# Two transformer blocks on one core: the scheduler's timing model exchanged, the program text unchanged

## The chip, the cores and the metric

The kernel runs on one core of a Trainium2 chip. The metric is the device time of one execution in microseconds; a comparison goes by the median of several runs. TensorE is called PE below, its weight loads PEld, VectorE DVE, ScalarE ACT, GpSimd POOL, SyncE SP.

## What is computed

One sequence of 512 tokens with 1024 features goes through two blocks of two layers each, all in float32. Cut to what matters:

```
first_block, per layer:                     # "block 1"
  u = rmsnorm(h) @ w_in                     # q, kv, rope, gates, GLA inputs
  y = [ MLA attention(u) * silu(gate_a),
        gated linear attention(u), two directions, chunks of 64, * silu(gate_g) ]
  h += y @ w_out
  h += sigmoid(rmsnorm(h) @ w_ple_gate) * (p @ w_ple_proj)
h = rmsnorm(h, final_norm)
second_block, per layer:                    # "block 2"
  u = rms_norm(h) @ w_in
  attn = dilated attention(rope(q), rope(k), v), three patterns, 8 heads
  dn   = gated delta rule(silu(conv(q, k, v))), 4 heads, chunks of 64:
         T = (I + A)^-1 by triangular solve, then a scan over 8 chunks
  h += rms_norm([attn, rms_norm(dn) * silu(z)] @ w_out)
  h += rms_norm((gelu(conv(gate)) * conv(up)) @ ffn_w_out)   # FFN of 2816
```

## The kernel before

Tokens lie in four tiles of 128 (`NT`); features are cut into eight blocks of 128 (`KT`). A float32 product is made from three matmuls of reduced type, in `mm3` (L178 to L181): high part by high part (L179), and the two mixed products (L180, L181). Operands are therefore split into a high part, cast on ACT (`split`, L263, and for weights L143), and a rest, subtracted on DVE (L264, L144).

Every weight comes through `take` (L130 to L146): SP issues a load of 512 KB into `wr` (L140, two buffers), ACT casts it to `wh` (L143), DVE subtracts to get `wl` (L144), four buffers each.

The places that the prediction speaks of, in the order of the program:

- `norm_t` (L329 to L340) normalizes one token tile in two halves: two squares with sums on ACT (L296), POOL forms the root (L297, L299), DVE writes `xn` (L335, two buffers, so that one tile at a time is held), and PE transposes it in eight pieces through `flip` (L274). The next tile's L296 writes its junk into the same `xn`.
- `gla_gate` (L495 to L509) of block 1: PE forms `ps_z` (L497), ACT takes absolute value, exponential and logarithm (L499 to L501) and the rest (L503), DVE adds and scans (L504 to L508).
- The delta rule of block 2. DVE solves 16 by 16 pieces in 30 dependent operations (L1043, L1045); ACT issues eight stores of them to the DRAM tensor `dT` (L1047). `q_rows` (L1051 to L1064) has short matmuls on `th`, a square that ACT makes (L1053 to L1056), and L1060, whose product DVE takes in L1061. `merges` (from L1104) loads T for one head back through ACT's queue (L1109), transposes it on PE (`ps_d`, L274), copies it on ACT (L1114), and builds the full inverse by L1120 to L1129. Then come the eight scan steps (L1145 to L1168): L1151 needs the state `S`; DVE adds (L1152); L1160 forms `ps_dS` from that; DVE adds it to the state (L1161), for the next L1151. L1154 and L1167 also use it, beside this chain.
- The set-up of the dilated attention (L1190 to L1195): ACT casts the keys (L1190), SP moves the halves across partitions (L1191), DVE subtracts (L1192), SP moves that (L1193). Scores are formed in L1220 and L1221.
- `add_norm` and `norm_t` for each token tile before the FFN, and the FFN itself.

What sets the order: each engine runs its own queue strictly in the order in which the instructions stand there, and waits at semaphores. That order isn't written by hand. The text gives each instruction a priority, its place in the program, which `tc.high_priority(offset=...)` moves forward; the scheduler steps through a timing model of the engines and lets each engine take, of what its model holds ready, what has the best priority. A few lines steer it:

```
with tc.high_priority(offset=lead[0]):        # every weight, in take()
...
with tc.high_priority(offset=600):
    oN = merges()
```

`lead[0]` is set stage by stage (30, 5, 80, ...), so weights come that much ahead of the work around them. The change touches `kernel`, L1446.

## Time and profile before

| | |
|---|---|
| median of 3 runs | 2128.76 us (2126.56 to 2129.99) |
| the profiled execution | 2130.51 us |
| its span, first to last instruction | 2128.4 us |
| mean granted TensorE clock | 0.996 |
| PE, PEld, DVE busy | 2037.4, 1685.4, 1279.2 us |
| ACT, POOL busy | 959.2, 194.9 us |
| DMA | 209.41 MB, 98 GB/s on the mean |

The sum in the prediction is made against the profiled execution, 1.75 us above the median. A matmul's duration in a row overlaps the next one's, since they are pipelined; the distance between two starts tells what one costs the queue.

### The profile page before, as it was taken

What the parts mean: (1) busy time and instruction counts of PE and PEld (TensorE: products, weight loads), DVE (VectorE), ACT (ScalarE), POOL (GpSimd) and SP (SyncE); (2) the same over time, 40 slices, a digit from 0 to 9 for tenths busy, and PEclk for the clock granted to TensorE, in tenths of its full rate; (3) what the DMA queues carried; (4) which work ended last, traced back from release to release, by engine and by line L of the source; (5) the groups of instructions that cost most, each with busy time, mean ns of one, the idle gap of its engine ahead of it and who ended that gap; (6) DMA issues with size and microseconds to landing.
All of it is one profiled execution on the core that took longest, in us unless ns stands there. A gap on an engine that the chain in (4) does not pass through costs nothing.

```text
span 2128.4 us, 28253 instructions
## 1 busy us (share of the span) xinstructions
PE 2037.4 (96%) x10792; PEld 1685.4 (79%) x10792; DVE 1279.2 (60%) x2218; ACT 959.2 (45%) x1805; POOL 194.9 (9%) x337
## 2 busy tenths in 40 slices
PE   7899999999999899999999999999999999999998
PEld 6687878778877888777788888878887678888886
DVE  6667655667844676575666425567757646662364
ACT  4745444635634553255544324346333654442342
POOL 1110001111000111200200000021112020000001
PEclk9999999999999999999999999999999999999999
DMA  5232233322133531141633333243211244332332
GB/s 170 85 92 70 70 109 118 104 80 87 44 127 103 173 95 58 45 114 51 188 109 99 92 96 99 70 152 113 79 55 50 75 146 142 99 97 92 99 99 89
DMA packets 74038, 209.41 MB, mean 98 GB/s; under 512 B 16624, under 2 KB 17648, under 8 KB 73392
## 3 DMA queue, kind: packets, MB, share of 16 engines
q1 hardware_dynamic: 62896, 202.89, 31.1%
q10 hardware_dynamic: 11008, 4.72, 0.9%
q8 instruction: 85, 1.39, 0.3%
q14 instruction: 49, 0.40, 0.1%
HBM read 182.16 MB, written 17.04 MB: 94 GB/s over the span
## 4 chain that ended last, share of the span: by engine, by line
PE 75%; DVE 7%; ACT 6%; DMA 5%; issue 3%; POOL 3%; POOLq 0%; SPq 0%; ACTq 0%; DVEq 0%
PE ps_mm L180 19%; PE ps_mm L181 18%; PE ps_mm L179 18%; DMA wr<-in_w 4%; DVE wl L144 2%; PE ps_tr L274 2%; ACT wh L143 2%; PE ps_o L1243 1%; ACT xn L296 1%; PE ps_mo L179 1%; PE ps_mo L180 1%; PE ps_pt L274 1%; PE ps_mo L181 1%; POOL r2h L297 1%; PE ps_pv L1151 1%
## 5 line engine op out<-in xcount | busy, mean ns | idle before, releaser
L144 DVE TENSOR_TENSOR wl<-wr,wh 128x1024 fp32r<-128x1024 f32 (+4 forms) x304 | 360.7, 1189 | 395.4 <-ACT wh L143 389.7
L143 ACT CAST wh<-wr 128x1024 fp32r<-128x1024 f32 (+4 forms) x304 | 309.3, 1019 | 357.1 <-PE ps_mm L181 151.3
L180 PE MATMUL ps_mm<-wl,xh 128*128 128x512 f32 (+2 forms) x736 | 282.6, 385 | 9.3 <-DVE wl L144 9.2
L181 PE MATMUL ps_mm<-x2h,wl 128*128 128x512 f32 (+1 forms) x768 | 285.5, 372 | 0.0
L180 PE MATMUL ps_mm<-x2l,wh 128*128 128x512 f32 (+1 forms) x768 | 285.4, 372 | 0.0
L179 PE MATMUL ps_mm<-x2h,wh 128*128 128x512 f32 (+1 forms) x768 | 285.4, 372 | 0.0
L179 PE MATMUL ps_mm<-wh,xh 128*128 128x512 f32 (+2 forms) x736 | 282.7, 386 | 2.1 <-ACT wh L143 1.7
L181 PE MATMUL ps_mm<-wh,xl 128*128 128x512 f32 (+2 forms) x736 | 280.9, 382 | 0.0
L180 PEld LDWEIGHTS ps_mm<-wl,xh 128*128 128x128 f32 x736 | 139.9, 190 | 37.5 <-DVE wl L144 15.0
L181 PEld LDWEIGHTS ps_mm<-x2h,wl 128*128 128x128 f32 x768 | 144.7, 188 | 25.1
L180 PEld LDWEIGHTS ps_mm<-x2l,wh 128*128 128x128 f32 x768 | 144.7, 188 | 25.0
L179 PEld LDWEIGHTS ps_mm<-x2h,wh 128*128 128x128 f32 x768 | 144.7, 188 | 24.9
L179 PEld LDWEIGHTS ps_mm<-wh,xh 128*128 128x128 f32 x736 | 139.5, 190 | 28.8 <-ACT wh L143 4.8
L181 PEld LDWEIGHTS ps_mm<-wh,xl 128*128 128x128 f32 x736 | 139.7, 190 | 23.3 <-issue 0.7
L1336 DVE SCALAR_TENSOR_TENSOR rt<-ps_mm,par,rt 128x511 f32<-128x511 f32 (+1 forms) x176 | 131.3, 746 | 3.0
L179 PE MATMUL ps_mm<-xh,wh 128*128 128x512 f32 x320 | 127.0, 397 | 0.9 <-DVE rp L358 0.9
L180 PE MATMUL ps_mm<-xl,wh 128*128 128x512 f32 x320 | 126.4, 395 | 0.0
L181 PE MATMUL ps_mm<-xh,wl 128*128 128x512 f32 x320 | 126.4, 395 | 0.0
L297 POOL TENSOR_SCALAR r2h<-ss 128x1 f32<-128x1 f32 x48 | 18.9, 393 | 995.0 <-ACT th L296 759.6
L180 PE MATMUL ps_mm<-wl,hh 128*128 128x512 f32 x224 | 89.1, 399 | 0.6 <-DVE wl L144 0.5
L179 PE MATMUL ps_mm<-wh,hh 128*128 128x512 f32 x224 | 88.2, 395 | 0.3 <-ACT wh L143 0.3
L181 PE MATMUL ps_mm<-wh,hl 128*128 128x512 f32 x224 | 88.0, 394 | 0.0
(401 smaller groups left out, 3798.3 us busy)
## 6 DMA issues: line engine op xcount, KB each, us to landing
wr<-in_w SPq DMA_DIRECT2D x270, 512.0 KB, 3.6
gain<-in_gain SPq DMA_DIRECT2D x13, 512.0 KB, 6.3
wr<-in_w SPq DMA_DIRECT2D x14, 384.0 KB, 3.1
x<-in_x SPq DMA_DIRECT2D x8, 512.0 KB, 5.9
wm<-gqk SPq DMA_DIRECT2D x32, 128.0 KB, 2.3
xd<-x SPq DMA_DIRECT2D x8, 512.0 KB, 2.6
xs<-xd SPq DMA_DIRECT2D x8, 512.0 KB, 3.9
xs<-xm SPq DMA_DIRECT2D x8, 512.0 KB, 4.6
```

The costliest lines, as they stand in the source:

```text
L143: nc.scalar.copy(hi[:, :n], raw[:, :n])
L144: nc.vector.tensor_tensor(lo[:, :n], raw[:, :n], hi[:, :n].bitcast(F32), ALU.subtract)
L179: nc.tensor.matmul(ps, l[0], r[0], start=start, stop=False)
L180: nc.tensor.matmul(ps, l[0], r[1], start=False, stop=False)
L181: nc.tensor.matmul(ps, l[1], r[0], start=False, stop=stop)
L274: nc.tensor.transpose(ps[:w, tsl(j)], src[:, tsl(j, w)], ident)
L296: nc.scalar.activation(junk[i], halves[i], AF.Square, accum_out=ss[:, i:i + 1])
L297: nc.gpsimd.tensor_scalar(r[:, i:i + 1], ss[:, i:i + 1], 1.0 / D, r[:, 0:1] if i else EPS, ALU.mult, ALU.add)
L1151: nc.tensor.matmul(pv[rs, tsl(h)], wT[h][:, cs], S[:, h], start=True, stop=True)
L1243: nc.tensor.matmul(o[tsl(h % 2, 64), tsl(h // 2)], av[:, j, tsl(h, 64)], p_[:, tsl(i * c + j)], start=j == 0, stop=j == qt)
L1336: nc.vector.scalar_tensor_tensor(acc[:, j:], ps[:, :SEQ - j], par[:, w0 + 3 * m + 2 - j:w0 + 3 * m + 3 - j], acc[:, j:], ALU.mult, ALU.add)
```

## The change

One argument of the context that schedules the program. The scheduler's model of time is another; the program text, its priorities, buffers and pools stay.

```diff
--- before.py
+++ after.py
@@ -1443,7 +1443,7 @@
     args["w"] = nc.dram_tensor("in_w", (W_TOTAL,), F32, kind="ExternalInput").ap()
     out = nc.dram_tensor("out_0", (P, NT, D), F32, kind="ExternalOutput").ap()
     plan = []
-    with tile.TileContext(nc) as tc, ExitStack() as ctx:
+    with tile.TileContext(nc, schedule_with_timeline_sim=True) as tc, ExitStack() as ctx:
         body(ctx, tc, args, out, plan)
     arrays["in_w"] = weight_stream(plan, I)
     r = _run(nc, [arrays], core_ids=[0])
```

Both programs have the same instructions, in the same numbers on every engine. The queues differ: of PE's, which has 8602 rows before when neighbours of one kind are put together and 8457 now, most stretches are in another order. The separate wait instructions also differ in number: 297 before and 259 now on PE, 503 and 539 on ACT, 462 and 496 on DVE, 371 and 359 on SP, 152 and 130 on POOL.

The first place is the scan of block 2's layer 0 on PE. Names with `ps_` are accumulators in PSUM: `ps_pv`, `ps_qv`, `ps_dS` and `ps_po` are the scan's, `ps_mm` belongs to the large products. Before:

```order
L181 MATMUL ps_mm<-wh,xl 128x512
L179 MATMUL ps_mm<-wh,xh 128x512
L1160 MATMUL ps_dS<-vn,kN 128x128 x4
L1167 MATMUL ps_po<-vn,ET 128x128 x4
L180 MATMUL ps_mm<-wl,xh 128x512
L1151 MATMUL ps_pv<-S,A 64x128 x4
L1154 MATMUL ps_qv<-S,qT 64x128 x4
L1160 MATMUL ps_dS<-vn,kN 128x128 x4
L274 MATMUL ps_tr<-ident,cv 128x128 x4
L181 MATMUL ps_mm<-wh,xl 128x512
L179 MATMUL ps_mm<-wh,xh 128x512
L1151 MATMUL ps_pv<-S,A 64x128 x4
```

and now:

```order
L1151 MATMUL ps_pv<-S,A 64x128 x4
L1160 MATMUL ps_dS<-vn,kN 128x128 x4
L1151 MATMUL ps_pv<-S,A 64x128 x4
L1154 MATMUL ps_qv<-S,qT 64x128 x4
L1160 MATMUL ps_dS<-vn,kN 128x128 x4
L1167 MATMUL ps_po<-vn,ET 128x128 x4
L1151 MATMUL ps_pv<-S,A 64x128 x4
L1154 MATMUL ps_qv<-S,qT 64x128 x4
L1160 MATMUL ps_dS<-vn,kN 128x128 x4
L1151 MATMUL ps_pv<-S,A 64x128 x4
L1154 MATMUL ps_qv<-S,qT 64x128 x4
L1160 MATMUL ps_dS<-vn,kN 128x128 x4
```

The products `ps_mm` that stood between the scan's own steps are gone from it; the scan's steps follow each other.

The second place is the first use of the inverse T on PE (`ps_d` from `dt`), with the products around it. Before:

```order
L181 MATMUL ps_mm<-wh,xl 128x512
L179 MATMUL ps_mm<-wh,xh 128x512
L274 MATMUL ps_tr<-ident,cv 128x128 x4
L180 MATMUL ps_mm<-wl,xh 128x512
L181 MATMUL ps_mm<-wh,xl 128x512
L180 MATMUL ps_mm<-wl,xh 128x512
L181 MATMUL ps_mm<-wh,xl 128x512
L274 MATMUL ps_d<-ident,dt 128x128 x4
L179 MATMUL ps_mm<-wh,xh 128x512
L180 MATMUL ps_mm<-wl,xh 128x512
```

and now:

```order
L179 MATMUL ps_mm<-xh,wh 128x512
L180 MATMUL ps_mm<-xl,wh 128x512
L181 MATMUL ps_mm<-xh,wl 128x512
L1056 MATMUL ps_tr<-ones,th 128x1 x4
L1060 MATMUL ps_tr<-qT,kT 128x128 x4
L1056 MATMUL ps_tr<-ones,th 128x1 x4
L274 MATMUL ps_d<-ident,dt 128x128 x4
L1060 MATMUL ps_tr<-qT,kT 128x128 x4
L1120 MATMUL ps_d<-dt 128x128 x4
L1056 MATMUL ps_tr<-ones,th 128x1 x4
L179 MATMUL ps_mm<-wh,xh 128x512
```

The transposes of T have moved into the middle of `q_rows` (L1056, L1060), ahead of the projection products that stood before them.

The third place is ACT's queue around the stores of T (L1047) and its load (L1109). Before:

```order
L143 CAST wh<-wr 128x1024
L969 ACTIVATE th<-cv 128x512
L964 ACTIVATE cv<-ps_mm,half_w 128x512
L1047 DMA dT_6505<-dt 16x16x16 x8
L143 CAST wh<-wr 128x1024
L969 ACTIVATE th<-cv 128x512
L1109 DMA dt<-dT_6505 128x512
L964 ACTIVATE cv<-ps_mm,half_w 128x512
L1114 COPY dt<-ps_d 128x512
```

and now:

```order
L1053 ACTIVATE th<-qT 128x512
L143 CAST wh<-wr 128x1024
L1047 DMA dT_6505<-dt 16x16x16 x8
L969 ACTIVATE th<-cv 128x512
L143 CAST wh<-wr 128x1024
L1109 DMA dt<-dT_6505 128x512
L1053 ACTIVATE th<-qT 128x512
L969 ACTIVATE th<-cv 128x512
L1053 ACTIVATE th<-qT 128x512
L969 ACTIVATE th<-cv 128x512
L964 ACTIVATE cv<-ps_mm,half_w 128x512
L1114 COPY dt<-ps_d 128x512
```

Two squares of `q_rows` (L1053) now stand behind the load of T, and one ahead of the stores.

## Rows read from the trace of the kernel before

**Rows 1.** The profile page, part 1: busy time, share of the span, instructions.

```profile
PE 2037.4 (96%) x10792; PEld 1685.4 (79%) x10792; DVE 1279.2 (60%) x2218; ACT 959.2 (45%) x1805; POOL 194.9 (9%) x337
```

**Rows 2.** Windows: stretch, its length, busy us and (count) by engine, PEclk, DMA share, GB/s.

```profile
13.00:712.00 699.00, 662.35 (x3575) 550.47 (x3576) 446.77 (x818) 347.05 (x707) 73.01 (x159) 0.99 0.31 97
712.00:1055.00 343.00, 327.33 (x1964) 270.29 (x1963) 223.62 (x472) 163.28 (x356) 48.11 (x63) 1.00 0.33 96
1200.00:1300.00 100.00, 100.00 (x438) 81.76 (x437) 31.35 (x32) 28.57 (x34) 0.00 (x0) 1.00 0.33 95
1395.00:1760.00 365.00, 346.61 (x2069) 284.49 (x2069) 243.82 (x500) 178.61 (x393) 60.36 (x85) 1.00 0.32 95
```

**Rows 3.** Waits of PE: what it waited for, us in total, times, longest us.

```profile
PE ps_tr L274 <- DVE xn L335: 32.7, 22, 7.4
PE ps_mm L180 <- DVE wl L144: 10.8, 17, 2.3
PE ps_mm L179 <- ACT wh L143: 3.9, 8, 0.9
PE ps_z L497 <- ACT wa L503: 3.6, 2, 2.4
PE ps_d L1129 <- DVE dt L1126: 3.6, 2, 1.8
PE ps_pv L1151 <- DVE S L1161: 2.7, 4, 0.8
...
PE ps_mm L179 <- DVE sga L364: 2.4, 2, 1.2
...
PE ps_d L274 <- DMA dt<-dT: 1.2, 2, 0.9
```

**Rows 4.** Timeline at 405 us, PE: start, us, line, operation, [idle before, releaser].

```profile
405.78 0.79 PE L180 MATMUL ps_mm<-wl,xh 128*128 128x512 f32 x1 [2.27 <-DVE wl L144]
...
406.37 0.63 PE L181 MATMUL ps_mm<-wh,xl 128*128 128x512 f32 x1
```

**Rows 5.** Windows: after that stall, and one stretch of the scan.

```profile
405.00:410.00 5.00, 4.22 (x12) 3.37 (x13) 4.85 (x6) 4.95 (x9) 3.32 (x4) 0.66 0.61 163
890.00:906.00 16.00, 15.30 (x104) 12.60 (x104) 9.91 (x17) 0.63 (x1) 5.32 (x6) 1.00 0.00 1
```

**Rows 6.** Timeline, solver end and T load, layer 0 (ACTq and SPq: DMA issues).

```profile
813.05 5.07 ACTq L1047 DMA_DIRECT2D dT<-dt  x8
...
820.43 0.36 ACTq L1109 DMA_DIRECT2D dt<-dT  x1
...
825.54 0.59 ACT L1114 COPY dt<-ps_d 128x512 f32<-128x512 f32 x1 [4.01 <-PE ps_d L274]
```

**Rows 7.** Timeline, scan of layer 0.

```profile
890.04 1.09 PE L1151 MATMUL ps_pv<-S,A 128*64 128x128 f32 x8 [0.75 <-DVE S L1161]
...
893.28 1.16 PE L1160 MATMUL ps_dS<-vn,kN 64*128 64x128 f32 x8
...
894.37 1.16 PE L1167 MATMUL ps_po<-vn,ET 128*128 128x128 f32 x8
894.54 0.69 DVE L1161 TENSOR_TENSOR S<-S,ps_dS 128x512 f32<-128x512 f32 x1 [1.23 <-PE ps_dS L1160]
```

**Rows 8.** Timeline, set-up before the attention of layer 0.

```profile
932.08 0.60 ACT L1087 ACTIVATE akT<-ps_tr 128x512 f32<-128x512 f32 x1 [3.38 <-PE ps_tr L274]
...
936.96 0.46 SPq L1193 DMA_DIRECT2D vs<-vs  x1
```

**Rows 9.** DMA of 934 to 948 us: issue, KB each, us to landing.

```profile
vs<-vs SPq DMA_DIRECT2D x1, 512.0 KB, 4.5
...
lo<-lo SPq DMA_DIRECT2D x1, 512.0 KB, 7.3
```

**Rows 10.** Timeline, two token tiles of the norm before the FFN.

```profile
1027.85 1.32 PE L274 MATMUL ps_tr<-ident,xn 128*128 128x128 f32 x8 [1.76 <-DVE xn L335]
...
1033.80 0.66 PE L274 MATMUL ps_tr<-ident,xn 128*128 128x128 f32 x4 [0.53 <-DVE xn L335]
```

## The prediction

> **What bounds the kernel now.** I read the busy times first: PE is busy 2037.4 us of the span of 2128.4 [rows 1], DVE 1279.2, ACT 959.2. So PE's queue sets the time, and a new order can only change how long PE stands idle and at which clock it runs. The windows tell where it stands: length less busy time is 36.7 us from 13 to 712 us (block 1), 15.7 from 712 to 1055 and 18.4 from 1395 to 1760 (the mixers of block 2 with the steps around them) [rows 2]. In the stretch of the FFN, 1200 to 1300, there is none: 438 matmuls in 100 us, so one costs 0.228 us. These 70.8 us are what a better order could win at most, apart from the clock. The list of PE's waits names them: 32.7 us for normalized rows, 10.8 and 3.9 us for the two halves of a weight, 3.6 us for the gate of block 1, 3.6 us in the merges, 2.7 us in the scan, and many groups like the 2.4 us for `sga` [rows 3].
>
> To these comes the clock. After 2.27 us idle at 405.78 us the next starts are 0.59 us apart and those after them 0.43, against 0.228 [rows 2, 4]: the level of 1.2 GHz. The 5 us from 405 on have a mean clock of 0.66 [rows 5], so 5 x 0.34 = 1.7 us of work is lost. The trace has four such places (near 68, 406, 436 and 713 us), each behind a stall of over 2 us.
>
> **The change part by part.** The instructions stay; only queues move. For each wait of PE I took from the two orders its cover: the matmul work that stands in PE's queue between the last matmul that the awaited value depends on and the matmul that waits, each at its undisturbed distance. A cover longer than the chain through ACT, DVE, POOL or DMA means no stall. The sum is made against the profiled execution, 2130.5 us; it lies 1.75 us above the median of the runs.
>
> *Gains.* The new order sets work that hangs on a chain later behind more products.
> - Weights, 14.7 us in 25 waits [rows 3]: of some 145 first waits on a new weight 26 had under 4 us of cover, now 8 of 141. I take 10 us; at least 5, at most 14.7.
> - The gate of block 1, 3.6 us [rows 3]: 3 of 6 covers were under 4 us, now none. 3.6 us.
> - L1129 in the merges, 3.6 us [rows 3]: 6 of 8 covers were under 1 us, now 1 of 7. 2.6 us.
> - Groups like `sga`, 2.4 us [rows 3], all in block 1 or at the start of the mixer: covers under 4 us were in the majority and are nearly gone. Together 12 us; bounds 6 and 14.
> - Normalized rows in block 1, part of the 32.7 us [rows 3]: 11 us of it is the start, when nothing else can run, and stays; at the later places covers grow by 2 to 5 us. 4 us; bounds 0 and 10.
> - Three of the four falls of the clock follow stalls that go: 3 x 1.7 = 5.1 us.
>
> Together -37.3 us.
>
> *Losses*, all in block 2, per layer twice.
> - The trip of T. The solver's last operations on DVE now stand behind an L1061, and that needs an L1060 which ends 7.7 us of matmuls before T's transposes. From there: about 1.9 us of DVE, then 7.4 us from the first store to the load (813.05 to 820.43), then 4.4 us until its data are in (the copy behind the transposes, which take 0.66, starts at 825.54) [rows 6]. That is 13.7 against 7.7: 6 us a layer, part of it already at the L1056 ahead, whose square stands behind that load on ACT. Before, both layers paid 1.2 us [rows 3]. Net +10.8; bounds 0 (everything earlier on DVE) and 14 (with a fall of the clock in each).
> - The scan. A step's L1160 starts at 893.28, L1161 at 894.54 and lasts 0.69, so the state is there 1.95 us on, while the queue can start the next matmul 1.09 us after L1160 (894.37) [rows 7]. With nothing between, 0.9 us is lost in each of the four steps without L1167 behind them, 3.6 us a layer. Before, products stood between, and L1151 still waited 0.75 us at 890.04 [rows 7]; 2.7 us in both layers [rows 3]. Net +4.5; bounds 0 and 10.
> - The set-up of the attention. From the copy of the last key tile (932.08) to the issue of the second move (936.96) it is 4.9 us, to its landing 4.5 more [rows 8, 9]: 9.4 us. The cover falls from 14.8 us to about 6.8: 2.6 us lost. The other half's rest lands only 7.3 us after its issue [rows 9]; what that costs, behind the first stall, lies between 0 and 5, and I take the middle, 2.5. Net +10; bounds 0 and 18.
> - The norm before the FFN. The transposes of the second tile now follow those of the first with nothing between; in the trace they start 5.95 us after them (1027.85 to 1033.80) [rows 10], of which eight transposes take 0.9. PE would wait 4.5 to 5 us and lose clock; but the four tiles stall for 5.0 us already before, and the third and fourth are better covered now. Net +2; bounds -4 and +8.
> - Covers that become very short elsewhere: 59 waits have under 0.5 us, 23 before. 24 of the 36 new ones are priced above; the others, at 0.4 us (the mean of those 23 without the start), and the operands of L179 and L181 in the first output product of each layer, come to +8; bounds 0 and 15.
>
> Together +35.3 us. I cost at nothing the FFN stretches, where PE is full and DVE and ACT have room [rows 2]; without that cover their weight waits would cost as in the list, some 5 us. The fewer wait instructions on PE (38) are worth at most 2 us, left out.
>
> By places the sum is -37.3 + 35.3 = **-2 us**. I do not trust this alone: it counts gains from stalls that were measured, and losses only where a chain is visibly longer than its cover. In the trace before, such chains explain about 60 of the 110 us that starts lie apart beyond their undisturbed distance at waits; the rest fell on waits with 2 to 10 us of cover. So I made a second sum, by classes: the mean stall of a wait before was 0.58 us below 0.5 us of cover, 0.11 at 0.5 to 2, 0.14 at 2 to 5, 0.12 at 5 to 10. Their counts go from 23, 190, 384 and 207 to 59, 153, 318 and 389. That gives 139 us now: **+29 us**. This sum does not know which chains are long. I take the middle, +13.5: 2130.5 + 13.5 - 1.75 = **2142 us** as a median.
>
> A rule on the clock speaks against the change. First the row: the scan's stretch from 890 to 906 us holds 0.7 us of idle time in pieces, and its clock is 1.00 [rows 5]. The Trainium skill, "TensorE: Matmul & The Clock Gate", section "A second HAM failure mode: psum-queue depth-cycling", says that short idle spells between groups of matmuls can make the clock swing between its levels. By the row the unfilled scan costs no clock; by the rule it is the fourth rival.
>
> **The rivals.**
> 1. *The trips in block 2 stay hidden*: faster. Both large losses rest on data that go through DRAM or across partitions and on when they are issued. If ACT and DVE reach the stores of T and L1190 earlier against PE, because PE itself was held up before, the stalls vanish. It decides at a trip of 7.7 us for T and 6.8 for the keys. For it: DVE is idle 40% and ACT 55% [rows 1]. Against it: 7.4 us of T's trip are issue and stores alone [rows 6]. 2142 - 10.8 - 10 = 2121 us.
> 2. *The sum by places is right*: 2130.5 - 2 - 1.75 = 2127 us. For it: every large wait of before was followed. Against it: the 50 us that no chain foretold.
> 3. *The classes are right, or more*: 2130.5 + 29 - 1.75 = 2158 us, up to 2172 where short covers cost more than their mean. For it: the shortest class grows from 23 to 59.
> 4. *The clock falls in the scan*: about 13 us of it a layer have nothing between the steps; at half the clock they take twice as long, 2 x 13 = 26 us: 2168 us. Against it stands the clock of 1.00 [rows 5].
> 5. *The orders amount to the same*: 2129 us. The two queues hardly share a stretch, so this would be chance.
>
> **How the numbers follow.** A measurement of this kernel can tell some 0.2%, 4.3 us, from no change. Chances: the forecast (2127 to 2158 as its own range) 0.36, of which 0.05 faster, 0.05 the same, 0.26 slower; rival 1 0.21 (0.20 faster, 0.01 same); rival 2 0.15 (0.08 faster, 0.07 same); rival 3 0.21, slower; rival 4 0.05, slower; rival 5 0.02, same. Faster 0.33, same 0.15, slower 0.52. The range takes in rival 1 down to 2112 (with the norms at their better bound) and rivals 3 and 4 to 2170.
>
> **What would show it.** Right: in the windows, less idle time of PE in block 1 (some 15 us in place of 36.7) and more in each mixer of block 2; in the waits, the groups for weights, `ps_z` and `sga` nearly gone; `ps_d` L274 or the L1056 ahead of it with about 6 us a layer, L1151 with four waits of 0.9 us a layer, L1220 or L1221 with 2 to 5 us; eight transposes behind eight with a stall of over 4 us. Clock 1.00 in the scan would reject rival 4. The forecast is wrong if block 2's mixers are idle no longer than before, or if block 1's stalls return under other names for the same sum.

## The result: slower, and the profile after

| | before | the change |
|---|---|---|
| median | 2129.38 us (2126.56 to 2131.05) | 2155.19 us (2148.09 to 2158.85) |
| ratio to before, 95% interval | | 1.0119 [1.0090, 1.0147] |
| profiled execution | 2130.51 us | 2148.09 us |
| its span, mean granted clock | 2128.4 us, 0.996 | 2146.3 us, 0.981 |

The change is slower by 25.8 us. The forecast was 2142 us (2112 to 2170), 13 us above before: the sign came true and the time lies inside the range, but the loss is twice the one that was forecast. The profiled execution is the fastest of four, so its trace can explain 17.6 us; the other 8 differ from run to run, in part with the clock, as shown below.

The profile page of the change, busy times (as [rows 1]):

```profile
PE 2046.5 (95%) x10792; PEld 1718.9 (80%) x10792; DVE 1287.1 (60%) x2218; ACT 949.2 (44%) x1805; POOL 191.5 (9%) x337
```

Windows of the change over the same four stretches of work (as [rows 2]; columns: stretch, its length, busy us and count of PE, PEld, DVE, ACT, POOL, clock, DMA share, GB/s):

```profile
13.00:709.00 696.00, 668.18 (x3572) 558.78 (x3572) 450.48 (x823) 342.64 (x708) 73.42 (x159) 0.99 0.31 98
709.00:1062.00 353.00, 328.85 (x1970) 281.46 (x1969) 225.15 (x466) 160.68 (x355) 45.50 (x63) 0.97 0.32 94
1200.00:1300.00 100.00, 100.00 (x439) 81.92 (x438) 31.50 (x32) 29.03 (x35) 0.00 (x0) 1.00 0.32 95
1402.00:1777.00 375.00, 346.13 (x2047) 294.84 (x2047) 248.60 (x502) 175.15 (x390) 58.06 (x84) 0.96 0.31 95
```

Length less busy time of PE: block 1 now stands idle 27.8 us in place of 36.7, the two mixers with their steps 24.2 and 28.9 in place of 15.7 and 18.4. The FFN is full as before. The two mixer stretches also lost clock: 0.97 and 0.96 in place of 1.00.

Waits of PE in the change (as [rows 3]: us in total, times, longest):

```profile
PE ps_tr L274 <- DVE xn L335: 19.5, 5, 7.8
PE ps_pv L1151 <- DVE S L1161: 7.0, 9, 0.9
PE ps_first L181 <- DVE xl L264: 6.0, 7, 2.2
PE ps_tr L1056 <- ACT th L1053: 5.4, 2, 2.7
PE ps_dS L1160 <- DVE vn L1152: 5.4, 7, 0.9
...
PE ps_mm L179 <- ACT x2h L263: 3.8, 2, 1.9
...
PE ps_s L1221 <- DMA lo<-lo: 1.2, 2, 0.7
...
PE ps_d L1129 <- DVE dt L1126: 0.8, 1, 0.8
...
PE ps_s L1221 <- DMA vs<-vs: 0.6, 1, 0.6
```

Six of these nine groups had no row among the waits of before: `xl` for `ps_first` (the first products of a layer), the square L1053, `x2h`, both moves of the keys, and L1160.

**Where the time went.** Both programs run the same matmuls, so there are points in PE's queue at which both have run exactly the same set. Distances between these points, from the starts of matmuls in the two profiled executions, in us:

| stretch | before | change | difference |
|---|---|---|---|
| block 1 and the step into block 2, up to its first products | 764.6 | 756.6 | -8.0 |
| mixer of layer 0 (projections, T, scan) | 168.9 | 177.1 | +8.2 |
| attention of layer 0 | 65.5 | 67.3 | +1.8 |
| norm before the FFN, layer 0 | 33.3 | 37.5 | +4.2 |
| FFN of layer 0 | 359.1 | 357.8 | -1.3 |
| step to layer 1 | 22.8 | 26.6 | +3.8 |
| first products of layer 1 | 62.4 | 58.8 | -3.6 |
| mixer of layer 1 | 169.6 | 175.3 | +5.7 |
| attention of layer 1 | 66.2 | 68.7 | +2.5 |
| norm before the FFN, layer 1 | 33.0 | 37.5 | +4.5 |
| FFN of layer 1 | 358.9 | 357.4 | -1.5 |

They sum to +16.3 of the 17.9 us by which the two spans differ; the rest lies ahead of the first point and behind the last. The stretches that lost have +30.7, the forecast's losses were +35.3; those that won have -14.4, the forecast's gains were -37.3. Each of these stretches is a net of what it won and lost.

### The profile page after: what moved, and what is told of

Same layout as the page of the kernel before. It is cut to its first block, busy times and chain, and to the rows that moved or that the text cites. A ratio compares the mean times of both kernels' runs of the same rounds, so it can differ in the third digit from the quotient of the medians.

```text
span 2146.3 us, 28251 instructions
## 1 busy us (share of the span) xinstructions
PE 2046.5 (95%) x10792; PEld 1718.9 (80%) x10792; DVE 1287.1 (60%) x2218; ACT 949.2 (44%) x1805; POOL 191.5 (9%) x337
## 4 chain that ended last, share of the span: by engine, by line
PE 84%; DVE 7%; ACT 4%; DMA 2%; issue 2%; POOL 2%; SPq 0%; DVEq 0%; POOLq 0%; ACTq 0%
PE ps_mm L180 21%; PE ps_mm L179 21%; PE ps_mm L181 21%; PE ps_tr L274 2%; PE ps_o L1243 1%; DVE wl L144 1%; DMA wr<-in_w 1%; PE ps_mo L181 1%; PE ps_pt L274 1%; PE ps_mo L179 1%; PE ps_first L181 1%; PE ps_mo L180 1%; PE ps_d L1120 1%; PE ps_d L1125 1%; POOL r2h L297 1%
## 5 line engine op out<-in xcount | busy, mean ns | idle before, releaser
L179 PE MATMUL ps_mm<-x2h,wh 128*128 128x512 f32 (+1 forms) x768 | 285.6, 375 | 3.8 <-ACT x2h L263 3.8
L179 PE MATMUL ps_mm<-wh,xh 128*128 128x512 f32 (+2 forms) x736 | 274.2, 381 | 2.8 <-ACT wh L143 2.0
L179 PEld LDWEIGHTS ps_mm<-x2h,wh 128*128 128x128 f32 x768 | 145.7, 191 | 29.8 <-ACT x2h L263 4.7
L180 PEld LDWEIGHTS ps_mm<-wl,xh 128*128 128x128 f32 x736 | 139.2, 189 | 28.9 <-DVE wl L144 5.4
L179 PEld LDWEIGHTS ps_mm<-wh,xh 128*128 128x128 f32 x736 | 138.7, 189 | 27.6 <-ACT wh L143 2.7
L179 PE MATMUL ps_mm<-xh,wh 128*128 128x512 f32 x320 | 126.6, 396 | 0.1
L179 PE MATMUL ps_mm<-wh,hh 128*128 128x512 f32 x224 | 87.0, 394 | 0.0
```

Of the source, the lines that this page charges most:

```text
L179: nc.tensor.matmul(ps, l[0], r[0], start=start, stop=False)
L180: nc.tensor.matmul(ps, l[0], r[1], start=False, stop=False)
```

## Experiments

Twelve runs, in three groups, each beside fresh runs of the kernel before on its chip (medians 2131.98, 2132.31 and 2132.26 us).

**The method.** A helper chains all instructions of each engine in a given order, by edges that only order the issue. So either program's order can be held, and also a mixture: each engine follows one order up to one of the points above and the other from there on.

```diff
-    with tile.TileContext(nc, schedule_with_timeline_sim=True) as tc, ExitStack() as ctx:
-        body(ctx, tc, args, out, plan)
+    with tile.TileContext(nc) as tc, ExitStack() as ctx:
+        body(ctx, tc, args, out, plan); hold(tc)
...
+def hold(tc):
...
+        row = [own[j] for j in np.cumsum(steps)]
...
+        for a, b in zip(row, row[1:]):
+            tc.add_manual_dep(b, a.name, info, reason="order")
```

What each mixture holds; all that isn't named is in the other order:

```
first_block_new    block 1 and its step to block 2: the change's order
second_block_new   all behind that:                 the change's order
mixers_new         both mixers with attentions:     the change's order
norms_new          both norms and the start of the
                   FFN behind, step to layer 1:     the change's order
mixers_old         both mixers with attentions:     the order of before
norms_old          both norms and the start of the
                   FFN behind, step to layer 1:     the order of before
best_mix           the change's order where its stretch was the shorter: most
                   of block 1 and the first products of layer 1
```

A second tool is *pads*: n extra matmuls of the identity with itself, ahead of a matmul that waits, into the bank that it is about to overwrite. Their products are never read. They are meant to keep PE busy through a wait, and so the clock up. The code is one line of the kernel, broken up here:

```diff
+        ps = psum.tile([P, 512], F32, tag=f"b{b[i]}", name=f"ps_{role}")
+        n, at = PADAT.get(CALLS[0], (0, 0))
...
+        PADS.extend((nc.tensor.matmul(ps[:, :P], ident, ident, start=True, stop=True).ins, at) for _ in range(n))
```

### Is it the clock? Pads in the change, in before, and in block 2 alone

`new_padded`: 188 pads at 55 waits of the change. 

> The order of the change, unchanged on every engine, with 188 extra small matmuls (identity by identity, 0.27 us each, results overwritten) put in PE's queue directly ahead of 55 matmuls that stand idle by 0.5 us or more in the profile of the change. They fill idle time and remove no wait. Theory A (the clock): the 26 us of the change are time at 1.2 GHz; with PE occupied in its stalls the clock stays up, so 2128 to 2138 us, mean clock 0.99 or more. Theory B (the waits): the new order's waits themselves are the loss and the clock only shows them; then 2150 to 2160 us, since every wait is still there.

`old_padded`: 144 pads at 46 waits of before, the control. 

> The same with the order of before: 144 small matmuls ahead of 46 stalls. Control for the price of the extra matmuls themselves. Theory A: before loses about 6 us to four falls of the clock, most of them behind stalls that can be filled, so 2123 to 2128 us. Theory B: 2129 to 2135 us, nothing to gain and some matmuls that come a little late.

`new_padded_2`: 142 pads at 26 waits, only in block 2. 

> The order of the change again, with extra small matmuls only in block 2 and only ahead of 26 matmuls that stood idle by 0.85 us or more (142 of them, counted at 0.25 us against the measured idle time, so that they end about with the wait): the norms before the FFN, the L1056 behind T, the scan, three products of the attention. new_padded raised the clock to 0.988 and won nothing, but its matmuls took 63.6 us where 45.4 us of idle time went, so 18 us were its own price. Theory A (the clock costs what it shows): about 12 us of the time at the low level in block 2 goes, 2139 to 2147 us. Theory B (the stalls are set by chains on ACT and DVE, and the clock falls inside them cost little): 2151 to 2160 us.

| | median us | ratio to before [95%] | clock of the profiled run |
|---|---|---|---|
| new_padded | 2153.72 (2151.19 to 2155.93) | 1.0101 [1.0087, 1.0115] | 0.988 |
| old_padded | 2131.84 (2128.06 to 2134.85) | 0.9998 [0.9989, 1.0008] | 0.995 |
| new_padded_2 | 2149.60 (2147.68 to 2150.96) | 1.0074 [1.0061, 1.0087] | 0.991 |

Pads change nothing in before, whose clock was 0.995 already. In the change they raise the clock. `new_padded` still came out at theory B's time: its pads took more than they gave. `new_padded_2`, whose pads are fitted more closely, lies between the two theories: it wins 8 to 10 us by the ratios, 1.0074 against 1.0119 and, in a later group, 1.0112, with intervals that don't meet. Even these pads aren't free: PE's idle time (the span less its busy time) falls from 99.8 us in the change to 78.1, by 21.7 us, but the pads themselves keep PE busy for 37.8. So the clock costs the change some 8 us or more; how much more can't be read from these runs.

Not all of the low clock costs something. The norm before the FFN of layer 1, in the windows of the change:

```profile
1764.00:1775.00 11.00, 5.89 (x25) 5.20 (x26) 9.67 (x15) 6.76 (x16) 4.92 (x12) 0.53 0.83 249
```

and of `new_padded_2`, the same work:

```profile
1767.00:1778.00 11.00, 8.61 (x69) 7.78 (x69) 9.42 (x13) 6.66 (x16) 4.68 (x12) 1.00 0.82 245
```

The clock rises from 0.53 to 1.00 and the stretch stays: 37.5 us in the change, 37.8 padded (layer 0: 37.5 and 39.0). In `new_padded` the same stretch took 37.5 us in both layers, at a clock of 1.00. The timeline of `new_padded_2` shows why:

```profile
1764.82 4.41 PE L120 MATMUL ps_tr<-ident 128*128 128x128 f32 x38
...
1769.94 1.32 PE L274 MATMUL ps_tr<-ident,xn 128*128 128x128 f32 x8 [0.72 <-DVE xn L335]
1771.10 1.95 PE L120 MATMUL ps_mm<-ident 128*128 128x128 f32 x16
...
1774.08 0.74 PE L179 MATMUL ps_mm<-x2h,wh 128*128 128x256 f32 x4 [1.03 <-ACT x2h L263]
```

A pad leaves two rows, as any float32 product does. With 19 pads (x38) through the wait for `xn` and 8 (x16) behind the transposes PE still waits 0.72 and 1.03 us at the ends: the chain through DVE and ACT sets this place, at either clock. The Trainium skill, "TensorE: Matmul & The Clock Gate", section "HAM oscillation — how this bites in real kernels", prices time at the lower clock at half its length; for these 11 us at 0.53 that would be some 5 us, an estimate. The trace doesn't agree: the measured price here is nothing.

### Which part? Blocks held apart

`first_block_new` 

> Block 1 up to the first products of block 2 in the order of the change on all engines, everything behind it in the order of before. By the two profiles the change is 8 us ahead at that point, with about as many falls of the clock as before: 2118 to 2125 us (theory A and B alike). The prediction's terms for block 1 alone would give some 2104 us.

`second_block_new` 

> The mirror: block 1 in the order of before, block 2 in that of the change. If the two halves add up, 2155 + 8 = 2163 us, 2156 to 2167. Theory A: mean clock at or below 0.985, with falls at the same places of block 2 as in the change. Theory B: clock near 0.99 and PE idle by 25 us more than before.

Measured: 2126.30 us (2123.50 to 2128.58), 0.9972 [0.9960, 0.9983], and 2161.73 us (2158.14 to 2164.44), 1.0138 [1.0124, 1.0152]. The new order of block 1 alone wins 5.7 us, and that of block 2 alone loses 29.8. They sum to +24.1, the whole has 24.8 to 25.8: the two blocks add up. So block 1's gain is real, but it is about a sixth of the gains that the forecast took (-37.3). The two theories on the clock weren't told apart here: `second_block_new` has the low clock of theory A (0.981) and also more idle time.

### Which part of block 2? Mixers and norms, both ways

`mixers_old` 

> The order of the change, but the two mixers of block 2 (merges, scan, set-up, attention; from L948 to the last attention product, both layers) in the order of before on all engines. Between places where both orders have run the same matmuls the profiles differ there by 8.2 + 1.8 us in layer 0 and 5.7 + 2.5 us in layer 1: 2155 - 18 = 2137 us, 2132 to 2142. The prediction's own terms for this place (T, scan, set-up, merges, short covers) sum to some 30 us, which would give 2125.

`norms_old` 

> The order of the change, but the norms around the FFN (second half of w_out with add_norm, in both layers, and the step from layer 0's FFN to layer 1) in the order of before on all engines. By the same comparison 4.2 + 3.8 + 4.5 us are lost there: 2155 - 12 = 2143 us, 2138 to 2148. The prediction gave these places 2 us in all, so 2153.

`mixers_new` 

> The order of before, with the two mixers of block 2 alone in the order of the change: the mirror of mixers_old. If the mixers lose what the profiles show at equal matmuls (8.2 + 1.8 + 5.7 + 2.5), 18 us above before; if, as in mixers_old, most of it hangs on how the stretch is entered, 8 to 12 us.

`norms_new` 

> The order of before, with the norms around the FFN alone in the order of the change: the mirror of norms_old. By the profiles 4.2 + 3.8 + 4.5 = 12 us above before; 2 us by the prediction's term.

`change_again`: the change once more, beside these. 

> The change itself once more, on the chip and in the call of the three below, for its interval: ratio 1.009 to 1.015 to before, as in the first four runs, and a spread of some 10 us that goes with the mean clock.

| | median us | ratio to before [95%] |
|---|---|---|
| mixers_old | 2147.00 (2144.39 to 2149.90) | 1.0062 [1.0050, 1.0075] |
| norms_old | 2153.78 (2151.44 to 2159.20) | 1.0091 [1.0075, 1.0106] |
| mixers_new | 2159.61 (2154.30 to 2162.19) | 1.0124 [1.0107, 1.0141] |
| norms_new | 2147.17 (2143.18 to 2148.15) | 1.0064 [1.0050, 1.0078] |
| change_again | 2157.05 (2152.49 to 2160.45) | 1.0112 [1.0094, 1.0129] |

Put into before, the mixers' order costs 27 us and that of the norms and the step 15; with block 1's -5.7 this is +36.6, more than the whole change's 25. Taken out of the change, each against its own runs of before, the mixers' order gives back 10 to 12 us; that of the norms gives back 3 to 6, with intervals that overlap the change's. Three of the four expectations that went by the profiles' stretches (18 us for the mixers, 12 for the norms) were missed; `norms_new` is 3 us off. So within block 2 the parts don't add up: 27 + 15 is more than the 29.8 of the whole block, 12 + 6 is less. The stretches show how, in us between the same points, each from one profiled execution (the two FFN stretches, 356 to 360 us in all of them, are left out):

```
                      before change again first_ mixers mixers norms norms cast_ new_pa best_
                                           block  new    old    new   old   first dded_2 mix
block 1, step, first   764.6  756.6 755.8  756.9  762.9  756.9 768.6 759.1 757.3  757.3 760.6
mixer, layer 0         168.9  177.1 177.0  170.9  175.7  173.4 168.9 179.4 181.9  179.9 169.9
attention, layer 0      65.5   67.3  67.5   66.2   67.6   66.6  65.5  67.8  67.5   67.6  65.2
norm, layer 0           33.3   37.5  37.5   33.6   33.7   37.7  37.0  34.0  35.2   39.0  32.9
step to layer 1         22.8   26.6  27.1   22.8   22.8   26.7  26.8  27.7  27.1   26.6  22.8
first products, layer 1 62.4   58.8  61.0   62.1   61.9   60.2  63.9  59.8  59.5   58.8  58.7
mixer, layer 1         169.6  175.3 176.7  169.8  181.1  175.9 169.6 181.1 181.1  174.9 173.7
attention, layer 1      66.2   68.7  69.6   67.3   67.9   68.6  66.2  69.7  69.7   67.3  67.3
norm, layer 1           33.0   37.5  37.0   33.1   36.1   36.7  37.0  37.4  35.4   37.8  33.3
```

The change's order of norms and step takes 37.0, 26.8 and 37.0 us even between neighbours in before's order (`norms_new`): they are 11.7 us longer than before, and that comes from the order inside. The reverse doesn't hold. Before's order of mixer and norm, entered from the change's, keeps before's time at one place of five: 34.0 us in the norm of layer 0 (`norms_old`); the step and the norm of layer 1 take 27.7 and 37.4 (`norms_old`), the mixers 173.4 and 175.9 (`mixers_old`). The granted clock is part of it: it is 1.00 in the norm of layer 0, but 0.88 in the step and 0.91 in the norm of layer 1, where before has 1.00; that is up to some 3 us in each (an estimate: 0.12 x 27.7 and 0.09 x 37.4). In the mixers the clock is 0.99, and PE stands idle for 7.5 and 8.8 us in place of 5.1 and 4.6. So the clock at which PE enters a stretch, and how far ACT and DVE have come by then, count beside the order inside; no run separates these, and it stays open.

### One suspected wait: two casts moved

In the change's queue on ACT the weight casts of the norm's stretch stand ahead of the casts of the second tile's transposes, for which PE waits. `cast_first` moves these ahead, and DVE's subtractions with them, in both layers; PE's order is the change's.

```diff
 L263 CAST x2h<-ps_tr 128x4x128
-L143 CAST wh<-wr 128x1024 x2
-L263 CAST x2h<-ps_tr 128x4x128
+L263 CAST x2h<-ps_tr 128x4x128 x3
+L143 CAST wh<-wr 128x1024 x2
...
-L263 CAST x2h<-ps_tr 128x4x128
```

> The order of the change with one place moved in each layer of block 2: at the norm of the second token tile before the FFN, the two casts L263 on ACT go ahead of the two weight casts L143, and the two subtractions L264 on DVE ahead of the two L144. PE's order is the same. Theory B (chains on ACT and DVE set the stall): the wait of the first FFN product (1.9 us) goes and this stretch falls from 37.5 us to about 35.5 in each layer, with the clock as low as before: 4 us under the change. Theory A (the clock): the stretch stays at 37 us or more as long as the clock falls there.

Measured: 2157.48 us (2151.82 to 2161.00), 1.0112 [1.0092, 1.0131], the same as the change. The place itself answered. The change, timeline in the norm of layer 0 (as [rows 10]):

```profile
1036.48 1.03 PE L274 MATMUL ps_tr<-ident,xn 128*128 128x128 f32 x8
...
1042.48 1.97 PE L274 MATMUL ps_tr<-ident,xn 128*128 128x128 f32 x8 [4.96 <-DVE xn L335]
...
1043.55 1.05 ACT L143 CAST wh<-wr 128x1024 fp32r<-128x1024 f32 x1 [2.87 <-DMA wr<-in_w]
...
1044.80 1.04 ACT L143 CAST wh<-wr 128x1024 fp32r<-128x1024 f32 x1 [0.20 <-DMA wr<-in_w]
...
1045.75 0.58 ACT L263 CAST x2h<-ps_tr 128x512 fp32r<-128x512 f32 x1
...
1046.38 1.23 PE L179 MATMUL ps_mm<-x2h,wh 128*128 128x256 f32 x4 [1.93 <-ACT x2h L263]
```

and `cast_first`:

```profile
1047.78 1.78 PE L274 MATMUL ps_tr<-ident,xn 128*128 128x128 f32 x8 [4.96 <-DVE xn L335]
...
1048.70 0.58 ACT L263 CAST x2h<-ps_tr 128x512 fp32r<-128x512 f32 x1 [2.72 <-PE ps_tr L274]
...
1049.34 0.80 PE L179 MATMUL ps_mm<-x2h,wh 128*128 128x256 f32 x2
```

ACT's casts of weights waited for DMA and held `x2h` back; now L179 starts 1.56 us behind the transposes in place of 3.90. With a new wait of 1.05 us for `wh` behind that, both norms became some 2.2 us shorter (35.2 and 35.4). But the total didn't move. In its profiled execution, the slowest of five, both mixers took 4.8 and 5.8 us longer than in the change's, the fastest of four, and the order in them is the same on every engine. Followed matmul by matmul, that time arises at two places of each layer where PE's clock was low for longer: behind the wait at L1056 (3.3 and 2.0 us; in layer 0 the clock from 810 to 820 us was 0.53, the change's 0.89), and in the scan (1.5 and 3.8 us). Windows of 36 us at the scan of layer 1, of the change, of `cast_first` and of `change_again`:

```profile
1624.00:1660.00 36.00, 29.05 (x219) 25.24 (x219) 23.97 (x37) 7.33 (x8) 9.88 (x12) 1.00 0.06 13
```

```profile
1634.00:1670.00 36.00, 29.91 (x195) 26.46 (x196) 22.66 (x36) 5.90 (x6) 9.88 (x12) 0.86 0.07 14
```

```profile
1630.00:1666.00 36.00, 29.82 (x205) 26.11 (x204) 26.02 (x37) 7.60 (x6) 9.59 (x12) 0.95 0.12 26
```

From its first L1151 to its last L1154 this scan took 33.5, 37.3 and 35.0 us, and the mixer of layer 1 175.3, 181.1 and 176.7; padded, at 1.00, 33.5 and 174.9. The scan of layer 0 in the change's own profiled execution fell too:

```profile
901.00:936.00 35.00, 29.44 (x210) 25.84 (x211) 23.47 (x37) 6.71 (x7) 9.85 (x12) 0.95 0.06 12
```

Six profiled executions hold the change's order of the mixers without pads, and in each the clock fell in at least one of the two scans (to a mean of 0.87 to 0.96); the two with pads and the six with the order of before have 1.00 in both. So the unfilled scan lets the clock fall, in some executions and not in others, and up to 3.8 us hang on it; with the place behind L1056 it is up to 6 us a layer. Whether the 4.4 us won in the norms reach the total can't be told: the intervals of `cast_first` and `change_again` are some 4 us to either side. Over the change's nine runs time goes with the clock, if not by it alone: 2148.09 and 2152.49 us at a mean clock of 0.981, 2154.44 and 2154.72 at 0.980, 2155.95 at 0.979, 2157.05 to 2160.45 at 0.976 and 0.977.

### A mixture of the shorter stretches

`best_mix` 

> For each stretch the order that was faster in its profile: the change's for block 1 (but before's for the MLA attention with the second output product of each layer) and for the first products of block 2's layer 1, before's for the mixers, the norms and the FFN. The stretches sum to 16 us under before: 2131 - 16 = 2115 us, 2110 to 2122, if stretches keep their times under other neighbours; 2126, as with the first block alone, if they don't.

Measured: 2128.19 us (2125.05 to 2134.07), 0.9984 [0.9972, 0.9995]. The mixture of shortest stretches wins no more than `first_block_new`, and the 2115 us were missed. A gain is partly borrowed: layer 1's first products take 58.7 us in place of 62.4, and the mixer behind them 173.7 in place of 169.6. The order in that mixer is before's, so its cover is the same; but PE comes to it 3.7 us sooner, and there it waits for two values that it did not wait for before (`th` of L1053 and `cv` of L966, 0.7 us each) and longer for T. The lowest median of all is that of `first_block_new`: the change's order in block 1, before's behind it.

## Why the prediction was right in sign and half in size

**The gains by places failed** (-37.3; the two stretches at which most of them lay gave -8.0 and -3.6). This is the step that made the forecast too small. By its terms block 1 alone would have brought the time to some 2104 us, 25 less; `first_block_new` measured a gain of 5.7. The named stalls did shrink, though less than put down: both halves of a weight from 14.7 to 7.2 us (forecast -10), `ps_z` from 3.6 to 2.1 (-3.6); L1129 fell from 3.6 to 0.8 (-2.6), and `sga` is gone, as said. The rows in block 1 shrank far more than the 4 us, 3.7 of it at the start, which the step had taken to stay. The waits of before from 13 to 712 us:

```profile
PE ps_tr L274 <- DVE xn L335: 13.0, 9, 3.7
...
PE ps_tr L274 <- DVE lgr L640: 2.6, 4, 1.1
```

and those of the change from 13 to 709 us:

```profile
PE ps_first L181 <- DVE xl L264: 3.5, 3, 2.2
PE ps_s L179 <- ACT e L755: 3.0, 3, 1.4
PE ps_sf L547 <- issue: 2.1, 1, 2.1
...
PE ps_kv L564 <- DVE amask L552: 1.9, 2, 1.1
PE ps_tr L274 <- DVE xn L335: 1.8, 2, 1.0
PE ps_first L179 <- ACT xh L263: 1.7, 3, 0.8
```

`xn` fell by 11.2 us, and `lgr` is gone. But new waits stand there: of `ps_first` for `xl` and `xh`, for `e` (exponentials of the MLA attention), and of the gated linear attention (`ps_sf`, `amask`); these five groups are 12.2 us, of which `xh` alone stood in the list of before, with 1.2. The step's mistake was to count a stall that goes as time won. It named no wait that would be late next in block 1. That block 1's stalls return under other names was the prediction's own sign of being wrong, and about half of them did: PE's idle time in the stretch fell from 36.7 to 27.8 us, where some 15 were foretold. The clock's part (-5.1) failed too: block 1 has 0.99 as before [rows 2], and the mixers lost clock on top.

**The norm was under-sized** (+2; measured +4.2 and +4.5, with the step to layer 1, for which no term stood, +12.5). The stall behind the first eight transposes is 4.96 us, as foretold (4.5 to 5), and the later tiles no longer wait. What was left out stands on ACT: the 1.93 us for `x2h` behind two weight casts, in each layer.

**The trip of T: right place, another chain, half the size** (6 us a layer). Timeline of the change, layer 0 (as [rows 6]):

```profile
797.57 4.12 ACTq L1047 DMA_DIRECT2D dT<-dt  x8
...
801.37 1.16 PE L1060 MATMUL ps_tr<-qT,kT 128*128 128x128 f32 x8 [0.26 <-DVE ssq L1057]
802.56 0.69 DVE L1061 TENSOR_TENSOR ET<-ps_tr,ET 128x512 f32<-128x512 f32 x1 [1.25 <-PE ps_tr L1060]
803.17 1.29 DVE L970 SCALAR_TENSOR_TENSOR qT<-th,cv 128x512 f32<-128x512 f32 x1
803.22 0.34 ACTq L1109 DMA_DIRECT2D dt<-dT  x1
...
804.56 0.63 ACT L1053 ACTIVATE th<-qT 128x512 f32<-128x512 f32 x1 [1.25 <-DVE qT L970]
...
805.24 1.83 PE L1056 MATMUL ps_tr<-ones,th 128*128 128x1 f32 x8 [2.72 <-ACT th L1053]
806.93 1.09 PE L274 MATMUL ps_d<-ident,dt 128*128 128x128 f32 x4
```

T's transposes don't wait. The stores start 9.36 us ahead of them: 5.65 us from the first store to the load and at most 3.71 from there, where the step had 7.4 and 4.4. But the trip is hidden behind another wait. Without the 2.72 us at L1056, PE would have come to the transposes at about 804.2, 1 us behind the load's issue, and the load took 3.2 us to land; some 2 us would have shown, an estimate from these rows. The stall is `q_rows`' own round: L1060 on PE, L1061 and L970 on DVE, L1053 on ACT, then L1056, with no product between. It costs 0.26 + 2.72 = 3 us a layer.

**The scan was under-sized in its waits** (net +4.5). Timeline of the change (as [rows 7]):

```profile
910.55 0.69 DVE L1172 TENSOR_REDUCE ss<-dt 128x4 f32<-128x512 f32 x1 [0.76 <-ACT dt L1170]
911.15 0.67 DVE L1152 TENSOR_TENSOR vn<-kT,ps_pv 64x512 f32<-64x512 f32 x1
...
911.88 1.16 PE L1160 MATMUL ps_dS<-vn,kN 64*128 64x128 f32 x8 [0.92 <-DVE vn L1152]
913.14 0.69 DVE L1161 TENSOR_TENSOR S<-S,ps_dS 128x512 f32<-128x512 f32 x1 [1.24 <-PE ps_dS L1160]
...
913.88 1.38 PE L1151 MATMUL ps_pv<-S,A 128*64 128x128 f32 x8 [0.85 <-DVE S L1161]
```

L1151 waits 0.78 to 0.85 us, as foretold (0.9), and once 0.40: nine times in all, 7.0 us. But there is a second wait, which the step put at nothing: L1160 for L1152, seven times, 5.4 us. It isn't the bare round from PE to DVE and back: the L1160 at 906.83, with L1154 ahead of it, doesn't wait. Ahead of the one at 911.88, DVE had a sum for the output's norm (L1172, for which it waited for ACT) in front of L1152 in its queue, and so at three more places; at two it was L1177, of the same norm. The seventh is the first step of layer 0, whose L1154 had run earlier. Together 12.4 us against the 2.7 of before: +9.7.

**The set-up of the attention was over-sized** (+10). Timeline of the change (as [rows 8, 9]):

```profile
937.37 0.46 SPq L1193 DMA_DIRECT2D vs<-vs  x1
...
941.53 0.62 PE L1221 MATMUL ps_s<-vs,A 128*128 128x256 f32 x3 [0.60 <-DMA vs<-vs]
...
945.64 0.46 SPq L1193 DMA_DIRECT2D lo<-lo  x1
...
949.80 0.39 PE L1221 MATMUL ps_s<-lo,qT 128*128 128x256 f32 x1 [0.50 <-DMA lo<-lo]
```

The wait came where it was put, with 0.6 and 0.5 us in place of 2.6 and 2.5. Both moves are there 4.2 us after their issue; the 7.3 us of [rows 9] for the second didn't come again.

**Short covers** (+8) were under-sized: `ps_first` alone, the first products of each layer, now waits 6.0 + 3.4 = 9.4 us for `xl` and `xh`, where 1.2 us were found before; others come on top, as 3.3 us for `mx` in the attention (0.6 before).

**The rivals.** Of the two sums, the one by classes of cover was right: +29 forecast, +25.8 measured (rival 3, 2158 us). It names no wait, and so leaves none out that is new; that it came within 3 us may be luck, since its mean stall knows nothing of DVE's queue or of the clock. Taking the middle between the two sums halved the result. Rivals 1 and 2 fall: T's trip was hidden and that of the keys nearly, as rival 1 said, but other rounds weren't. Rival 4, the clock in the scan, came true in part: 0.95 in layer 0 and 1.00 in layer 1 of the profiled execution, down to 0.87 in others, at up to 3.8 us a layer in place of 26 for both. The rule cited with it, the Trainium skill's "TensorE: Matmul & The Clock Gate", section "A second HAM failure mode: psum-queue depth-cycling", agrees with the 0.86 of `cast_first` and not with the 1.00 of layer 1 in the change's profile.

## What to carry to other kernels

When a new order removes named stalls, ask for each what stands late behind it; where that can't be traced, the count of covers by length, priced at the mean stall of before, was the better sum in this one case, and the average of the two had no ground of its own. In a recurrence, price every round trip from PE to another engine and back, not only the one that carries the state, and look at what stands ahead of it in the other engine's queue. An order that is chosen stretch by stretch has to be timed as a whole: a stretch that PE reaches sooner finds the other engines less far.

## What the runs showed of the hardware that was not expected

The same order of the same scan (layer 1) ran at a granted clock of 1.00, 0.95 and 0.86 in different executions, with idle pieces of under 1 us, and took 33.5, 35.0 and 37.3 us. And a low clock can be free: at 0.53 or at 1.00 the norm's stretch took 37.5 or 37.8 us, since PE stood in a chain through DVE and ACT either way.
